# A hybrid trunk layer in which HGRN's key-value products share the scores' pair of PSUM banks and seven heads' outputs are scaled a step later

## The chip, the core and the metric

The kernel runs on one core of one Trainium2 chip. The metric is device time in microseconds (us); less is better. A core has TensorE (PE, with its weight loads as PEld), VectorE (DVE), ScalarE (ACT), GpSimd (POOL) and SyncE (SP), which here only issues DMAs. Each engine works through its own instructions in a fixed order and waits on semaphores for the others. PE writes into PSUM, of which the kernel uses eight banks of 128 partitions × 512 float32; DVE and ACT read the banks out.

## The reference

One decoder layer on x of 1024 tokens × 1024 channels, float32. Its token mixing has two branches, HGRN2 (8 heads, key and value width 128) and a retention (4 heads), which are gated, merged and projected; a squared-ReLU MLP follows. The change concerns HGRN2, whose recurrence in the reference goes over chunks of 64 tokens:

```python
def step(state, blk):
    qc, lfc, kc, vc = blk
    b = jnp.cumsum(lfc, axis=2)
    rel = jnp.where(causal, b[:, :, :, None, :] - b[:, :, None, :, :], -jnp.inf)
    scores = jnp.einsum('bhid,bhijd,bhjd->bhij', qc, jnp.exp(rel), kc)
    b_last = b[:, :, -1:, :]
    o = (jnp.einsum('bhij,bhje->bhie', scores, vc)
         + jnp.einsum('bhid,bhde->bhie', qc * jnp.exp(b), state))
    state = (jnp.exp(b_last[:, :, 0, :, None]) * state
             + jnp.einsum('bhjd,bhje->bhde', kc * jnp.exp(b_last - b), vc))
    return state, o
...
o = _head_norm(_from_chunks(o), centered=False).reshape(B, S, HG_WIDTH)
return (o * jax.nn.silu(g.astype(f32))).astype(g.dtype)
```

`_head_norm` divides each token's 128 outputs of a head by the root of their mean square. Scores, outputs and states of a head are what the words "scores", "outputs", "products" and "state" mean below; a product is the key-value sum that is added to the decayed state.

## The kernel before, in words

The dense projections run as three passes over hi and lo halves of the float32 operands (`mm3`, L188 to L190), in groups of 24 matmuls of 128x512 into a bank "d". Weights arrive in float32 and are split by ACT (L183) and DVE (L184). PSUM is handed out by `ps` under four letters, each with a number of banks that its tiles take in turn: "d" 3, "a" 2, "b" 1, "c" 2. A tile takes the bank of the tile that many places before it under the same letter, and its first write waits until that one's readers are done. In SBUF a pool of 15 half-row tiles (`e`) rotates in the same manner; loads that take such a tile wait until its last reader is done.

HGRN works in chunks of 128 tokens, eight of them a head, one head after another. `h_levels` computes a head's scores with the decay inside the chunk taken up level by level. The first level (L883) and two more (L935) are 32 small matmuls each, in which four groups of 32 rows work on one "a" bank; DVE copies the wanted entries out under a mask (L886, L887, L941) into a tile C. The last level (L923) fills two "a" banks of 32 small matmuls in all, which ACT copies out (L927). Between the levels DVE rescales queries and keys (L908 to L955).

`h_states` then takes the head's eight chunks in turn. For chunk n PE adds query times state (L991) and scores times values (L992) into a "c" bank `po`; ACT copies that out (L993) and squares it with a sum over each token (L994). For all but the last chunk PE multiplies turned keys and values (L997) into a bank `pu`, also "c", and DVE makes the new state of it: a copy for the first chunk (L1000), else old state times decay plus product (L1002). The keys are turned by four transposes (L973) into the "b" bank, once for each half of four chunks, and copied out by ACT (L975); the half's gate is loaded from DRAM by SP (L969).

At a half's last chunk DVE scales the mean squares (L1007) and POOL raises them to the power −1/2 (L1008). Two steps then follow with delays, counted in steps of the stream: `h_scale`, in which ACT scales the four output tiles (L1014), and `h_out`, in which PE transposes them into the "b" bank (L1024), DVE multiplies by the gate (L1028) and POOL stores them (L1029). The table `H_DEFER` holds both delays, one pair for heads 0 to 6 and one for head 7 (`H_DEFER[h // 7]`).

`h_stream` runs nine steps a head: at each step one chunk of the head before, one part of the levels of this head, then `tick`, which releases what is due. The stream is mixed at build time with dense projections (`h_fill`), the projection of the retention's finished outputs (`r_first`, L1341 and L1342) and the beginning of the retention's second head (`r_head`, whose loads of rq and rk are L1155 and whose transposes of the keys are L1167, into "a"). That is the order in which the program is written; a scheduler then sets each engine's final order from the instructions' dependences, its own estimates of their durations, and the order written. Instructions outside this stage keep their order in the change.

Of the kernel before, what the change touches and what calls it, by code (L numbers as in the profile page):

```python
# [19 lines left out]
P = 128  # L20
# [37 lines left out]

ADA_ORDER = [(s, g) for s in (S_GATE2, S_GATE1, S_SCALE2, S_SHIFT2) for g in range(4)]

H_DEFER = ((1, 2), (2, 3))
H_STEPS = 9


# [70 lines left out]
class Trunk:  # L135
# [824 lines left out]
    def h_states(self, p, hd):  # L960

        nc = self.nc
        h = 2 * p + hd
        s = self.hst[p][hd]
        k, v, Q, S, Dt = s["k"], s["v"], s["Q"], s["S"], s["D"]

        def turned(hf):
            g = self.e2()
            nc.sync.dma_start(g, self.hg_d[h][:, hf * 512:hf * 512 + 512])  # L969
            pb = self.ps("b")  # L970
            for c in range(4):
                cs = slice(hf * 512 + c * P, hf * 512 + c * P + P)
                nc.tensor.transpose(pb[:, c * P:(c + 1) * P], k[:, cs], self.ident)  # L973
            kt = self.e2()
            nc.scalar.activation(kt, pb, AF.Copy)  # L975
            return g, kt

        state = None
        nxt = turned(0)
        yield  # L980
        for hf in (0, 1):
            g, kt = nxt
            ob, sq = (self.e2().rearrange("p (c e) -> p c e", c=4) for _ in (0, 1))
            mr = self.xp.tile([P, 8], F32, tag="ms", bufs=2, name=self.uid("ms"))
            ms, rs = mr[:, :4], mr[:, 4:]
            for c in range(4):
                n = 4 * hf + c
                vn = v[:, n, hd * P:(hd + 1) * P]
                po = self.ps("c", (P, P))
                if n > 0:  # L990
                    nc.tensor.matmul(po, Q[hf][:, c * P:(c + 1) * P], state, start=True, stop=False)  # L991
                nc.tensor.matmul(po, S[:, n, :], vn, start=n == 0, stop=True)  # L992
                nc.scalar.activation(ob[:, c, :], po, AF.Copy)  # L993
                nc.scalar.activation(sq[:, c, :], ob[:, c, :], AF.Square, accum_out=ms[:, c:c + 1])  # L994
                if n < 7:
                    pu = self.ps("c", (P, P))
                    nc.tensor.matmul(pu, kt[:, c * P:(c + 1) * P], vn, start=True, stop=True)  # L997
                    ns = self.xp.tile([P, P], F32, tag="st", bufs=2, name=self.uid("st"))
                    if n == 0:
                        nc.vector.tensor_copy(ns, pu)  # L1000
                    else:
                        nc.vector.scalar_tensor_tensor(ns, state, Dt[:, n:n + 1], pu, op0=ALU.mult, op1=ALU.add)  # L1002
                    state = ns
                if n == 2:
                    nxt = turned(1)
                if c == 3:
                    nc.vector.tensor_scalar(ms, ms, 1.0 / P, HEAD_EPS, op0=ALU.mult, op1=ALU.add)  # L1007
                    nc.gpsimd.tensor_tensor(rs, ms, self.mhalf[:, :4], op=ALU.pow)  # L1008
                    self.later(H_DEFER[h // 7][0], lambda ob=ob, rs=rs, hf=hf, g=g: self.h_scale(h, hf, ob, rs, g))
                yield  # L1010

    def h_scale(self, h, hf, ob, rs, g):
# [4 lines left out]
        self.h_last = r  # L1017
        self.later(H_DEFER[h // 7][1], lambda: self.h_out(h, hf, ob, g))

# [856 lines left out]
```

## Time and profile before

| | us |
|---|---|
| median of 3 runs (2230.02 to 2231.53) | 2231.18 |
| the profiled execution | 2231.17 |
| its span in the profile | 2229.4 |
| PE busy outside the HGRN stage's later part, 0 to 912 us | 893.37 |
| PE busy from 1181 us to the end | 1032.34 |

The span leaves out 1.8 us around the profiled work. The last two rows are sums over windows of the profile: PE was busy for 893 of the first 912 us, and for 1032 of the last 1048. The mean granted clock of PE was 0.997 of full speed. A profile gives for each engine the time that it was busy, groups of instructions by source line and tile names (buffer numbers left out), the idle time before an instruction with the instruction that released it, and windows with the busy time and clock inside each. A group's "x64" counts records: a float32 matmul has two passes, and so two records.

### The profile page before, as it was taken

The page shows a single profiled execution, that of the slowest core. Times are in us where ns is not written, and L with a number is a line of the kernel's source. Part 1 is how long each engine was busy: PE and PEld are TensorE (multiplying, and loading weights), DVE is VectorE, ACT ScalarE, POOL GpSimd, SP SyncE. Part 2 cuts the span into 40 slices and gives each one's busy share as a digit, 9 for nine tenths or more (in the row PEclk, how much of TensorE's full clock was granted, in tenths as well). Part 3 has the DMA queues.
Part 4 walks back from the last instruction along what each step waited for, and adds up shares of the span by engine and source line. Part 5 has one row for each costly group of instructions (what it writes and reads, how often), then busy time and mean ns, then how long its engine had stood idle before and what let it go on. Part 6 is the DMA issues. An engine that isn't in the chain of part 4 may idle for free.

```text
span 2229.4 us, 32724 instructions
## 1 busy us (share of the span) xinstructions
PE 2188.0 (98%) x11879; PEld 1798.3 (81%) x11879; DVE 1577.7 (71%) x2756; ACT 1050.6 (47%) x1954; POOL 302.4 (14%) x468
## 2 busy tenths in 40 slices
PE   7999999999999999999999999999999999999998
PEld 5888888888888887888787888888888888788886
DVE  7866768686777637767756656687796665667778
ACT  5433334544333435555656545223565555643441
POOL 0111111011111113010022222031111211100001
PEclk9999999999999999999999999999999999999999
DMA  9766755543333355222237657764344444877863
GB/s 285 236 227 229 243 191 172 170 147 114 107 110 102 136 176 199 91 86 91 90 121 247 225 180 272 241 212 135 111 156 156 151 149 154 303 249 255 257 216 118
DMA packets 229378, 396.29 MB, mean 178 GB/s; under 512 B 17992, under 2 KB 123200, under 8 KB 228448
## 3 DMA queue, kind: packets, MB, share of 16 engines
q1 hardware_dynamic: 198464, 294.34, 41.3%
q0 software_dynamic: 30576, 99.79, 12.1%
q8 instruction: 93, 1.52, 0.3%
q14 instruction: 69, 0.57, 0.1%
q10 hardware_dynamic: 176, 0.06, 0.0%
HBM read 289.26 MB, written 104.87 MB: 177 GB/s over the span
## 4 chain that ended last, share of the span: by engine, by line
PE 88%; issue 3%; DVE 3%; DMA 2%; ACT 2%; POOL 1%; SPq 0%; DVEq 0%; ACTq 0%; POOLq 0%
PE psd L188 17%; PE psd L189 17%; PE psd L190 17%; PE psa L188 5%; PE psa L189 5%; PE psa L190 5%; PE psc L189 3%; PE psc L188 3%; PE psc L190 3%; PE psb L1247 2%; PE psb L188 2%; PE psb L189 2%; PE psb L190 1%; PE psc L1233 1%; PE psa L1181 1%
## 5 line engine op out<-in xcount | busy, mean ns | idle before, releaser
L188 PE MATMUL psd<-U,wh 128*128 128x512 f32 x696 | 279.3, 404 | 0.8 <-ACT U L183 0.7
L189 PE MATMUL psd<-U,wh 128*128 128x512 f32 x696 | 275.7, 396 | 0.3 <-DVE U L184 0.3
L190 PE MATMUL psd<-U,wl 128*128 128x512 f32 x696 | 275.2, 396 | 0.0
L183 ACT ACTIVATE bh<-s 128x512 fp32r<-128x512 f32 x212 | 133.1, 633 | 252.7 <-PE psd L189 64.6
L188 PE MATMUL psd<-U,bh 128*128 128x512 f32 x528 | 205.5, 389 | 2.0 <-DVE e L450 2.0
L183 ACT ACTIVATE bh<-raw 128x512 fp32r<-128x512 f32 x159 | 100.9, 637 | 224.2 <-PE psd L189 92.7
L189 PE MATMUL psd<-U,bh 128*128 128x512 f32 x528 | 205.5, 389 | 0.1
L190 PE MATMUL psd<-U,bl 128*128 128x512 f32 x528 | 205.4, 389 | 0.0
L184 DVE TENSOR_TENSOR bl<-raw,bh 128x512 fp32r<-128x512 f32 x159 | 108.5, 689 | 121.5 <-ACT bh L183 121.0
L184 DVE TENSOR_TENSOR bl<-s,bh 128x512 fp32r<-128x512 f32 x212 | 144.4, 686 | 64.9 <-ACT bh L183 64.9
L188 PEld LDWEIGHTS psd<-U,wh 128*128 128x128 f32 x696 | 131.3, 189 | 28.0 <-ACT U L183 2.8
L190 PEld LDWEIGHTS psd<-U,wl 128*128 128x128 f32 x696 | 131.8, 189 | 27.1
L189 PEld LDWEIGHTS psd<-U,wh 128*128 128x128 f32 x696 | 132.0, 190 | 26.9 <-DVE U L184 1.7
L183 ACT ACTIVATE U<-hr 128x512 fp32r<-128x512 f32 x112 | 70.3, 630 | 146.2 <-issue 75.5
L188 PEld LDWEIGHTS psd<-U,bh 128*128 128x128 f32 x528 | 99.1, 188 | 23.4 <-DVE e L450 2.8
L189 PEld LDWEIGHTS psd<-U,bh 128*128 128x128 f32 x528 | 99.1, 188 | 21.0 <-DVE U L184 0.5
L190 PEld LDWEIGHTS psd<-U,bl 128*128 128x128 f32 x528 | 99.1, 188 | 20.5
L184 DVE TENSOR_TENSOR U<-hr,U 128x512 fp32r<-128x512 f32 x112 | 77.0, 688 | 53.8 <-ACT U L183 53.4
L183 ACT ACTIVATE wh<-raw 128x512 fp32r<-128x512 f32 (+1 forms) x79 | 57.1, 740 | 101.3 <-PE psd L189 84.0
L188 PE MATMUL psa<-U,bh 128*128 128x512 f32 x264 | 102.9, 390 | 0.8 <-ACT e L438 0.8
L189 PE MATMUL psa<-U,bh 128*128 128x512 f32 x264 | 102.7, 389 | 0.0
L190 PE MATMUL psa<-U,bl 128*128 128x512 f32 x264 | 102.7, 389 | 0.0
(453 smaller groups left out, 5437.6 us busy)
## 6 DMA issues: line engine op xcount, KB each, us to landing
raw<-in_w_in SPq DMA_DIRECT2D x146, 512.0 KB, 4.3
raw<-in_w_down SPq DMA_DIRECT2D x64, 512.0 KB, 4.0
raw<-in_w_ada SPq DMA_DIRECT2D x32, 512.0 KB, 4.7
raw<-in_w_up SPq DMA_DIRECT2D x32, 512.0 KB, 3.9
raw<-in_w_pb SPq DMA_DIRECT2D x20, 512.0 KB, 4.4
v_d<-e POOLq DMA_DIRECT2D x32, 256.0 KB, 4.4
rg_d<-e POOLq DMA_DIRECT2D x32, 256.0 KB, 2.6
e<-v_d SPq DMA_DIRECT2D x32, 256.0 KB, 5.0
```

What stands on the lines that cost most here:

```text
L183: self.nc.scalar.activation(hi, src, AF.Copy)
L184: self.nc.vector.tensor_tensor(lo, src, hi.bitcast(F32), op=ALU.subtract)
L188: r = mm(out, wh, uh, start=start, stop=False, skip_group_check=more)
L189: mm(out, wh, ul, start=False, stop=False, skip_group_check=more)
L190: return r, mm(out, wl, uh, start=False, stop=stop, skip_group_check=more)
L1181: m = nc.tensor.matmul(pa[:, cs], k[e][:, cs], q[e][:, cs], start=e == 0, stop=e == 1)
L1233: mm(G[e], l[:, n % 2, es], r, start=n == 0 and i == 0, stop=i == 2, skip_group_check=n > 0)
L1247: mm(po, l, r, start=i == 0, stop=i == len(pairs) - 1)
```

## The change

Two edits. The product's bank `pu` is taken from the letter "a" instead of "c": the "a" pair then holds scores and products in turn, and the "c" pair the chunk outputs alone (and, after this stage, what the retention puts there). And the delay of `h_scale` of heads 0 to 6 goes from one step to two; that of `h_out` behind it stays at two, and head 7 is as before.

```diff
-H_DEFER = ((1, 2), (2, 3))
+H_DEFER = ((2, 2), (2, 3))
...
                 if n < 7:
-                    pu = self.ps("c", (P, P))
+                    pu = self.ps("a", (P, P))
                     nc.tensor.matmul(pu, kt[:, c * P:(c + 1) * P], vn, start=True, stop=True)
```

No instruction is added or removed. The scheduler gives PE, DVE, ACT, POOL and SP new orders within the HGRN stage. Three places on PE; a name's number counts tiles, and "x21" is a run of equal rows.

PE where chunks 2 and 3 of head 0's states run beside a level of head 1's scores (L935). Before:

```order
L997 MATMUL psc_8335<-U_7793,e_8145 128x128
L935 MATMUL psa_8367<-U_7790,fk_7802 32x48 x21
L991 MATMUL psc_8358<-st_8337,e_8130 128x128
L992 MATMUL psc_8358<-U_7793,U_7785 128x128
L935 MATMUL psa_8367<-U_7790,fk_7802 32x48 x10
L997 MATMUL psc_8363<-U_7793,e_8264 128x128
L935 MATMUL psa_8367<-U_7790,fk_7802 32x48
```

And in the changed kernel:

```order
L997 MATMUL psa_8335<-U_7793,e_8145 128x128
L997 MATMUL psa_8359<-U_7793,e_8264 128x128
L188 MATMUL psd_8417<-U_296,wh_7975 128x512
L189 MATMUL psd_8417<-U_297,wh_7975 128x512
L190 MATMUL psd_8417<-U_296,wl_7976 128x512
L991 MATMUL psc_8354<-st_8337,e_8130 128x128
L992 MATMUL psc_8354<-U_7793,U_7785 128x128
L935 MATMUL psa_8363<-U_7790,fk_7802 32x48 x32
```

The second product moves up to the first, three dense matmuls come between it and the next output, and the level's 32 matmuls stand in one piece.

PE where head 6's states begin, head 7's first scores (L883) are computed, and the outputs of head 5's second half are transposed (L1024); psd is a dense projection. Before:

```order
L992 MATMUL psc_10757<-U_7794,U_7785 128x128
L997 MATMUL psc_10761<-U_7794,e_10709 128x128
L883 MATMUL psa_10765<-hq_7792,fk_10496 32x3x16 x32
L1024 MATMUL psb_10800<-cst,e_10525 128x128 x4
L188 MATMUL psd_10808<-U_10714,wh_10268 128x512
```

And in the changed kernel:

```order
L992 MATMUL psc_10757<-U_7794,U_7785 128x128
L997 MATMUL psa_10761<-U_7794,e_10705 128x128
L883 MATMUL psa_10765<-hq_7792,fk_10492 32x3x16 x32
...
L190 MATMUL psd_10800<-U_10729,wl_10265 128x512
L991 MATMUL psc_10816<-st_10763,e_10690 128x128
L992 MATMUL psc_10816<-U_7794,U_7785 128x128
L997 MATMUL psa_10821<-U_7794,e_10705 128x128
L1024 MATMUL psb_10834<-cst,e_10521 128x128 x4
```

The transposes move behind twelve dense matmuls (the last of them is shown) and the next chunk's output and product.

PE near the end of the stage, where the retention's keys are transposed (L1167) into two "a" banks behind the last head's products. Before:

```order
L997 MATMUL psc_11295<-U_7794,e_11163 128x128
L1167 MATMUL psa_11301<-cst,e_11211 128x128
L1167 MATMUL psa_11301<-cst,e_11212 128x128
L1167 MATMUL psa_11301<-cst,e_11211 128x128
L1167 MATMUL psa_11301<-cst,e_11212 128x128
L1167 MATMUL psa_11308<-cst,e_11211 128x128
```

And in the changed kernel, in which psa_11308 has the bank that psa_11295 had:

```order
L997 MATMUL psa_11295<-U_7794,e_11159 128x128
L1167 MATMUL psa_11301<-cst,e_11203 128x128
L1167 MATMUL psa_11301<-cst,e_11204 128x128
L1167 MATMUL psa_11301<-cst,e_11203 128x128
L1167 MATMUL psa_11301<-cst,e_11204 128x128
L188 MATMUL psd_11334<-U_10714,wh_10734 128x512
L1167 MATMUL psa_11308<-cst,e_11203 128x128
```

A dense matmul now stands between the two groups of four.

## The prediction

> **What bounds the kernel now.** I read the page first: how busy each engine is, and the chain of work that ended last.
>
> ```profile
> span 2229.4 us, 32724 instructions
> PE 2188.0 (98%) x11879; PEld 1798.3 (81%) x11879; DVE 1577.7 (71%) x2756; ACT 1050.6 (47%) x1954; POOL 302.4 (14%) x468
> PE 88%; issue 3%; DVE 3%; DMA 2%; ACT 2%; POOL 1%; SPq 0%; DVEq 0%; ACTq 0%; POOLq 0%
> ```
>
> TensorE (PE) is busy for 98% of the span and carries 88% of the chain. So an edit is worth what it takes from PE: idle time of PE, time that PE runs at a lower clock, or PE time spent badly. Next, the stage that the change touches, from about 912 to 1181 us, as a whole and around its longest wait. Columns: window; its length; then busy us and count of PE, weight loads, DVE, ACT, POOL; the granted PE clock; DMA share; GB/s.
>
> ```profile
> 912.00:1181.00 269.00, 262.27 (x2988) 217.80 (x2988) 172.77 (x395) 151.30 (x451) 37.66 (x46) 0.99 0.30 100
> 1117.00:1119.00 2.00, 1.77 (x7) 1.15 (x8) 0.53 (x1) 1.62 (x7) 0.59 (x1) 0.97 0.29 113
> 1119.00:1122.20 3.20, 3.20 (x9) 2.49 (x8) 3.06 (x9) 0.00 (x0) 0.55 (x1) 0.50 0.24 93
> 1122.20:1126.00 3.80, 3.80 (x21) 3.25 (x20) 0.47 (x3) 1.17 (x4) 0.54 (x1) 0.99 0.18 69
> ```
>
> PE is idle for 269.00 − 262.27 = 6.7 us of the stage; DVE is busy 64% and ACT 56% of it, so neither is a bound over the stage. From 1119.0 to 1122.2 PE ran at clock 0.50. Then PE's waits in the same window (us in total, times, longest):
>
> ```profile
> PE psb L1024 <- ACT e L1014: 3.2, 3, 1.7
> PE psc L991 <- DVE st L1002: 1.2, 4, 0.5
> PE psc L997 <- ACT e L975: 1.1, 3, 0.6
> PE psa L923 <- DVE U L955: 0.5, 1, 0.5
> PE psa L935 <- DVE U L909: 0.3, 1, 0.3
> ```
>
> These are 6.3 of the 6.7 us. The longest, followed back through the timelines (start, duration, then the idle time before it and who ended it):
>
> ```profile
> 1114.34 0.39 PE L997 MATMUL psc<-U,e 128*128 128x128 f32 x2
> 1114.66 0.89 PE L883 MATMUL psa<-hq,fk 128*32 128x48 f32 x64
> 1117.23 1.21 PE L1024 MATMUL psb<-cst,e 128*128 128x128 f32 x4 [1.69 <-ACT e L1014]
> 1114.57 0.16 DVE L1007 TENSOR_SCALAR ms<-ms 128x4 f32<-128x4 f32 x1
> 1114.82 1.92 POOL L1008 TENSOR_TENSOR ms<-ms,small 128x4 f32<-128x4 f32 x1 [9.79 <-DVE ms L1007]
> 1116.78 1.28 ACT L1014 ACTIVATE e<-e,ms 128x128 f32<-128x128 f32 x4 [1.85 <-POOL ms L1008]
> ```
>
> The chain is DVE L1007, then 1.92 us of POOL's power L1008, then ACT's scaling L1014, then the transposes. PE reached the transposes at 1117.23 − 1.69 = 1115.54 and stood for 1.69 us, and the half clock follows right behind.
>
> **Change, part 1: scaling a step later.** The order of this place is the second of those shown with the change: the transposes leave the place right behind L883. Twelve dense matmuls and a chunk's three products (L991, L992, L997) now run first. What that is worth, from the rows:
>
> ```profile
> 959.08 0.39 PE L189 MATMUL psd<-U,wh 128*128 128x512 f32 x1
> 959.30 0.39 PE L190 MATMUL psd<-U,wl 128*128 128x512 f32 x1
> 959.53 0.38 PE L991 MATMUL psc<-st,e 128*128 128x128 f32 x2
> 959.75 0.39 PE L992 MATMUL psc<-U,U 128*128 128x128 f32 x2
> 959.97 0.39 PE L997 MATMUL psc<-U,e 128*128 128x128 f32 x2
> ```
>
> A dense matmul starts 0.22 to 0.23 us after the one before, and so does a product (two passes each). Twelve and three are 15 × 0.225 = 3.4 us of new cover against a wait of 1.69. The other two waits sum to 3.2 − 1.7 = 1.5 us, each under it. **Term: −3.2 us** (bounds 0 and −3.2).
>
> With the wait goes the half clock. The window at 1119.0 has 3.20 us at 0.50, that is 1.6 us of work lost. **Term: −1.6** (bounds 0 and, with the transposes that ran into it, −2.1). The page "TensorE: Matmul & The Clock Gate" of the Trainium skill, in Part 1, has the gate look at activity in free-running windows of 3413 ns, and its closing table ("Why this matters for your kernels") asks only that no idle gap exceed about 3 us; by that rule a gap of 1.69 us costs no clock, the term is nothing, and the sum would be 1.6 us smaller. The trace disagrees as to the size: here 0.50 stands behind 1.69 us.
>
> The scaling's other effects: as many ACT instructions are issued as before, and the transposes, DVE's multiplication by the gate (L1028) and POOL's store (L1029) come a step later, off the chain. But the scaled tile, the gate tile and their rotating places in the pool of 15 come free later. The order on SP shows one consequence: the retention's load of rq (L1155) now takes the place of head 6's second output tile, and so waits for its transposes; behind it on SP queue one rq, two rk and hg loads.
>
> ```profile
> 1151.67 1.01 SPq L1155 DMA_DIRECT2D e<-rk_d  x2
> 1159.11 1.04 PE L1167 MATMUL psa<-cst,e 128*128 128x128 f32 x8
> ```
>
> Before, 6.4 us lay between the last rk issue (1152.68) and the transposes L1167 of the retention's keys that read it, and L1167 waited for nothing. How early the loads landed inside those 6.4 us is not seen here, and the group of transposes that they now wait for takes 0.6 to 1.2 us (1.21 at the half clock above): I take **+0.8**, nearer to the side of no wait (bounds 0 and +3, if the whole 6.4 us were needed and the issue came half a step of PE's work later).
>
> **Part 2: the products move to the scores' banks.** Before, outputs and products shared two "c" banks, so every product waited for the copy of the output before it and each output for a state update; now the outputs have both. The products (L997) take turns with the scores (L883, L935, L923) in two "a" banks. The first order shown with the change has what follows.
>
> A product no longer waits behind an output's copy, so it is issued early, and the small score matmuls stay in one piece. The price of splitting them is in the trace; a whole set first, then one that two groups of products split:
>
> ```profile
> 891.79 0.89 PE L935 MATMUL psa<-U,fk 128*32 128x48 f32 x64
> 892.61 0.50 PE L188 MATMUL psd<-U,wh 128*128 128x512 f32 x1
> ...
> 960.29 0.70 PE L935 MATMUL psa<-U,fk 128*32 128x48 f32 x42
> 961.17 0.49 PE L991 MATMUL psc<-st,e 128*128 128x128 f32 x2 [0.18 <-DVE st L1002]
> 961.50 0.39 PE L992 MATMUL psc<-U,U 128*128 128x128 f32 x2
> 961.81 0.45 PE L935 MATMUL psa<-U,fk 128*32 128x48 f32 x20
> 962.19 0.49 PE L997 MATMUL psc<-U,e 128*128 128x128 f32 x2
> 962.61 0.27 PE L935 MATMUL psa<-U,fk 128*32 128x48 f32 x2
> 962.81 0.50 PE L188 MATMUL psd<-U,wh 128*128 128x512 f32 x1
> ```
>
> In one piece the 64 passes take 892.61 − 891.79 = 0.82 us. Split twice they and three products take 962.81 − 960.29 = 2.52 us; less 0.82, less three products at 0.22, less the idle 0.18, 0.86 us are left, 0.43 for each interruption. Counted over the stage, the order has the scores in 59 pieces before and 44 after. Most of the fifteen cut a set as here, some move only an edge, so I take 0.32 each: **−4.9** (bounds: nothing, if the time belongs to the products, and 15 × 0.43 = −6.4).
>
> The three waits of L997 for L975 (the copy of the turned keys) sum to 1.1 us. After the change those products find the copy done, since PE does other things first: **−1.1** (bounds 0, −1.1). The four waits of L991 for the state update L1002 sum to 1.2 us. By start-to-start times of the rows above, 14 of 56 places before have under 0.8 us of PE work between product and the next use of the state, 4 after. In the group at 923 us three instructions, not one, delay the state:
>
> ```profile
> 923.30 0.63 ACT L183 ACTIVATE wh<-raw 128x512 fp32r<-128x512 f32 x1 [5.38 <-PE psd L189]
> 923.97 0.69 DVE L184 TENSOR_TENSOR wl<-raw,wh 128x512 fp32r<-128x512 f32 x1 [1.76 <-PE psc L992]
> 924.58 0.34 DVE L1002 SCALAR_TENSOR_TENSOR st<-st,D,psc 128x128 f32<-128x128 f32 x1
> ```
>
> The update stood behind the weight's split (L184), so some of the wait stays: **−0.6** (bounds 0, −1.2).
>
> **New waits on the "a" pair.** A product now waits for DVE's masked copies of the scores that held its bank, and scores wait for the update that reads a product. The longest such reads:
>
> ```profile
> L941 DVE COPY_PREDICATED hC<-mask,psa 128x128 f32<-128x128 uint8 x42 | 13.2, 315 | 3.1 <-PE psa L935 3.0
> ```
>
> Three copies are 0.95 us; the order leaves at least 2.2 us of PE work (estimated from the rows' start-to-start times) between scores and the product that takes their bank, at 14 places. An update is 0.34 us; the order leaves 0.45 and 0.9 us at the two tightest of 14 places where L923 follows, and one dense matmul, 0.23 us, besides the first group ahead of the second group of transposes L1167 (the third order shown). I put 0.4 on that last, 0.3 on the 0.45, 0.3 on the rest: **+1.0** (bounds 0 and +6, that is 0.4 at each of the 15). Behind a product that waits, PE holds everything.
>
> **Sum**: −3.2 −1.6 −4.9 −1.1 −0.6 +0.8 +1.0 = −9.6 us. The profiled execution took 2231.17 us and the median of the runs is 2231.18, so the sum applies unchanged: **2221.5 us**.
>
> **Rivals.** *The gain is mostly hidden.* The time in the split sets belongs to the products that follow small matmuls and not to the split, or the fewer pieces come back as waits on banks. Then −4.9 falls away and new waits cost 2 us more: −9.6 + 4.9 + 2.0 = −2.7, **2228.5 us**. For it: this one split set carries the price. Against: the split set's own pieces are longer, passes and products alike (0.49 against 0.39).
>
> *The "a" pair becomes the tight resource.* This one ends slower. It decides when DVE finishes the third masked copy later than 2.2 us behind the scores: three copies (0.95) and one weight split (0.69) in its queue make 1.64 and fit; a second split ahead of them, 2.33, is just too late, and a third operation of that length makes it 3.02 and the wait 0.8. Then 14 products behind L935 wait 0.8 us each, 11.2, the 7 behind L883 (with two copies to wait for) half of that, 2.8, and two such waits end in a half clock, 3.2 us. With −11.4 from what is removed and +0.8 from the loads, that is +6.6: **2238 us**. In "Perfetto Trace Analysis", section "Matmuls", the Trainium skill has independent matmul groups rotate through different banks, so that reading one out overlaps the next group; by that, putting three kinds of work in one pair speaks against this change, and the sum would be this rival's. The trace bears it out only in part: L935 and L923 waited 0.8 us in all before, and never for a bank.
>
> *The deferral does nothing*: DVE issues L1007 later behind its copies, POOL's power ends as much later, and PE stands again where the transposes are now. Then 3.2 + 1.6 stay: −4.8, **2226.4 us**. Against: L1007 would have to slip by the 3.4 us of new cover, ten times an update's 0.34.
>
> **How the numbers follow.** Forecast, including the cases near it, 0.64; deferral without effect 0.05; hidden 0.21; tight pair 0.10. The forecast's own ends: all gains at their bounds and no new wait, −3.2 − 2.1 − 6.4 − 1.1 − 1.2 = −14, 2217; the tops of the new waits in part, about 2227. The range reaches to 2215.5 below, for a wait that goes without being counted here (L923 and L935, 0.8), and to 2231 above, past the hidden rival. A measurement of this kernel can tell about 0.2%, 4.5 us, from no change, so faster means under 2226.7: 0.68. Same, between 2226.7 and 2235.6: 0.23. Slower: 0.09.
>
> **What would show it.** In the profile after: no wait of L1024 for L1014 in the stage before head 7; no half clock near 1120 us; L935 rows of x64 in most groups, and the stage's end (L1167 behind it) about 9 us earlier. A row "psa L997 <- DVE hC" of over 5 us would show the tight pair; a wait of L1167 for the rq or rk load the SP term. The forecast is wrong if PE's busy time in the stage doesn't fall by 4 us or more: then the pieces were no cost.

## The result and the profile after

The changed kernel takes 2218.26 us (median of 3 runs, 2217.57 to 2218.39), before 2231.18: a ratio of 0.9941, 95% interval 0.9928 to 0.9955, some 12.9 us less. Of all the runs in this document one, of the deferral alone, took 3789.64 us at a mean granted clock of 0.634, for a cause that isn't known; the ratios leave it out, and the median of that kernel's other ten is 2226.48. The profile of the changed kernel is of an execution of 2217.57 us. Its page, span, busy time by engine and the chain by engine:

```profile
span 2215.8 us, 32734 instructions
PE 2180.3 (98%) x11879; PEld 1792.3 (81%) x11879; DVE 1575.5 (71%) x2756; ACT 1049.3 (47%) x1954; POOL 301.5 (14%) x468
PE 90%; DVE 3%; DMA 3%; ACT 2%; issue 1%; POOL 0%; SPq 0%; DVEq 0%; ACTq 0%; POOLq 0%
```

The same work takes 7.7 us less of PE's busy time (2188.0 before), and the span is 13.6 us shorter. To see both on equal terms, one window each from the stage's first L883 to the same PE instruction near its end; first before, then after (columns as in the prediction):

```profile
886.67:1174.27 287.60, 280.87 (x3303) 232.33 (x3303) 190.51 (x433) 156.99 (x465) 36.28 (x44) 0.99 0.31 102
```

```profile
887.19:1161.85 274.66, 273.39 (x3304) 227.19 (x3304) 190.28 (x433) 156.29 (x465) 34.97 (x44) 1.00 0.33 108
```

The stretch is 12.94 us shorter. Its idle time of PE fell from 287.60 − 280.87 = 6.73 to 1.27, by 5.5 us. Its busy time fell by 7.5; 1.7 of that is the half clock, which the stretch of before has once (3.41 us at 0.50) and that of after not at all. 5.8 us are left: the same matmuls, done in less time. PE's waits in the stage after (912 to 1170 us):

```profile
PE psc L991 <- DVE st L1002: 0.5, 1, 0.5
PE psc L991 <- DVE st L1000: 0.5, 1, 0.5
```

Nothing else is left of the 6.3 us of before, and no wait names a bank. The place where PE stood for 1.69 us, in the timeline of after:

```profile
1107.20 0.89 PE L883 MATMUL psa<-hq,fk 128*32 128x48 f32 x64
1108.02 0.50 PE L188 MATMUL psd<-U,wh 128*128 128x512 f32 x1
...
1111.32 0.39 PE L997 MATMUL psa<-U,e 128*128 128x128 f32 x2
1111.54 0.60 PE L1024 MATMUL psb<-cst,e 128*128 128x128 f32 x4
1111.89 0.48 PE L188 MATMUL psd<-U,wh 128*128 128x512 f32 x1
```

The transposes start without an idle time behind the dense matmuls and products, and take 0.35 us. And a whole score set beside the chunk's products, where before had it in three pieces:

```profile
959.98 0.89 PE L935 MATMUL psa<-U,fk 128*32 128x48 f32 x64
960.80 0.49 PE L991 MATMUL psc<-st,e 128*128 128x128 f32 x2
961.12 0.39 PE L992 MATMUL psc<-U,U 128*128 128x128 f32 x2
961.35 0.39 PE L997 MATMUL psa<-U,e 128*128 128x128 f32 x2
```

The 64 passes take 0.82 us, with one way in and one way out. The retention's loads, which now wait for a tile of head 6, and the transposes that read them:

```profile
1133.02 1.71 SPq L1155 DMA_DIRECT2D e<-rq_d  x2
1136.33 4.41 SPq L1155 DMA_DIRECT2D e<-rk_d  x2
```

```profile
1146.92 0.60 PE L1167 MATMUL psa<-cst,e 128*128 128x128 f32 x4
1147.27 0.48 PE L188 MATMUL psd<-U,wh 128*128 128x512 f32 x1
1147.60 0.60 PE L1167 MATMUL psa<-cst,e 128*128 128x128 f32 x4
```

The last rk load is issued by 1140.74, 6.2 us ahead of L1167, and L1167 waits for neither the load nor the bank.

### The profile page after: what moved, and what is told of

It reads as the page before. It is cut to its first block, busy times and chain, and to the rows that moved or that the text cites. A ratio compares the mean times of both kernels' runs of the same rounds, so it can differ in the third digit from the quotient of the medians.

```text
span 2215.8 us, 32734 instructions
## 1 busy us (share of the span) xinstructions
PE 2180.3 (98%) x11879; PEld 1792.3 (81%) x11879; DVE 1575.5 (71%) x2756; ACT 1049.3 (47%) x1954; POOL 301.5 (14%) x468
## 4 chain that ended last, share of the span: by engine, by line
PE 90%; DVE 3%; DMA 3%; ACT 2%; issue 1%; POOL 0%; SPq 0%; DVEq 0%; ACTq 0%; POOLq 0%
PE psd L188 17%; PE psd L189 17%; PE psd L190 17%; PE psa L190 5%; PE psa L189 5%; PE psa L188 5%; PE psc L189 3%; PE psc L188 3%; PE psc L190 3%; PE psb L1247 2%; PE psb L188 1%; PE psb L189 1%; PE psb L190 1%; PE psc L1233 1%; PE psa L1181 1%
## 5 line engine op out<-in xcount | busy, mean ns | idle before, releaser
L183 ACT ACTIVATE bh<-s 128x512 fp32r<-128x512 f32 x212 | 133.2, 633 | 253.2 <-PE psd L189 65.5
L183 ACT ACTIVATE bh<-raw 128x512 fp32r<-128x512 f32 x159 | 100.9, 637 | 224.0 <-PE psd L189 92.4
L184 DVE TENSOR_TENSOR bl<-raw,bh 128x512 fp32r<-128x512 f32 x159 | 108.4, 689 | 121.1 <-ACT bh L183 120.5
L184 DVE TENSOR_TENSOR bl<-s,bh 128x512 fp32r<-128x512 f32 x212 | 144.4, 686 | 66.3 <-ACT bh L183 66.1
L183 ACT ACTIVATE U<-hr 128x512 fp32r<-128x512 f32 x112 | 70.4, 630 | 144.7 <-issue 75.5
L184 DVE TENSOR_TENSOR U<-hr,U 128x512 fp32r<-128x512 f32 x112 | 77.0, 687 | 53.0 <-ACT U L183 52.6
L183 ACT ACTIVATE wh<-raw 128x512 fp32r<-128x512 f32 (+1 forms) x79 | 57.1, 740 | 98.8 <-PE psd L189 79.8
```

Of the source, the lines that this page charges most:

```text
L183: self.nc.scalar.activation(hi, src, AF.Copy)
L184: self.nc.vector.tensor_tensor(lo, src, hi.bitcast(F32), op=ALU.subtract)
```

## The experiments

All ran beside runs of before. Their medians were 2231.17 us for the two single edits and the two kernels with split sets, 2232.30 for the two that move the step within the deferral, and 2231.26 for the other four. Edits are shown against the changed kernel unless said otherwise.

**Each edit alone.** The bank alone:

```diff
-H_DEFER = ((2, 2), (2, 3))
+H_DEFER = ((1, 2), (2, 3))
```

> The bank change alone; the scaling stays one step behind. Counted over the stage its order has the scores in 42 pieces (before 59, both edits 44). If the parts add as in my working, the fewer pieces and the waits of L991 and L997 are won here, about 5.7 and 2 us, and the waits of L1024 for L1014 stay, about 3 us, with a half clock behind one of them or not: 2223 to 2224. Rival, the deferral does nothing: as fast as both edits, 2218. Rival, the pieces are no cost: 2228 to 2229.

2227.15 us, ratio 0.9982 (0.9973 to 0.9991). That misses the expected range by 3.2 us and lies nearer to the rival by which the pieces are no cost; the windows below and the pair with the extra product speak against that rival. The deferral alone:

```diff
-                    pu = self.ps("a", (P, P))
+                    pu = self.ps("c", (P, P))
```

> The deferral alone; the products stay in the outputs' banks. 60 pieces of scores, as before. If the parts add: the waits of L1024 for L1014 go, 3.2 us, and up to 3.4 us of lost clock with them, while the waits of L991 and L997 stay: 2225 to 2228. Rival, the deferral does nothing: 2231.

2226.89 us, ratio 0.9978 (0.9969 to 0.9987), within the expected range. The windows of the same stretch, the bank alone first, then the deferral alone:

```profile
885.73:1166.55 280.82, 274.77 (x3303) 226.79 (x3303) 190.62 (x433) 156.55 (x465) 36.09 (x44) 1.00 0.31 106
```

```profile
886.33:1168.04 281.71, 278.69 (x3304) 231.09 (x3303) 190.89 (x433) 156.22 (x465) 35.84 (x44) 1.00 0.31 105
```

The two edits take from different columns. Without the half clock, before has 280.87 − 1.71 = 279.16 us of busy PE. The bank takes 4.4 us of it (42 pieces) and leaves 6.05 us idle; the deferral takes 0.5 (60 pieces) and leaves 3.02 us idle. Of PE's waits with the bank alone, up to 1160 us, those of the transposes are the longest:

```profile
PE psb L1024 <- ACT e L1014: 4.1, 3, 1.7
```

These were 3.2 us before: PE comes to the transposes sooner (for head 1's first half 0.8 us after DVE starts the last L1007, and 1.5 in before), while POOL's power ends 1.8 us after that start in both, so part of what the banks win is lost again in the wait that the other edit removes. The profiled execution of the bank alone was the fastest of its eleven runs (2223.24), so its window says which column moves, and the median how much.

**Is the whole more than the parts?** The kernel with both edits once more:

> The kernel with both edits, unchanged, beside the runs of before on one chip, to set against each edit alone (4.0 and 4.3 us by the medians). If both edits together are worth more than the sum, as the first comparison has it (12.9 against 8.3): 2217 to 2219. If that was the luck of three runs: 2222 to 2223.

2219.16 us, ratio 0.9949 (0.9937 to 0.9962), in the first of the expected ranges but for 0.2 us. The product of the ratios of the two single edits is 0.9960, and the intervals overlap; so by the medians a gain beyond the sum is likely, but its size isn't shown. In the windows of the stretch the parts take 4.4 + 0.5 us of busy time and 0.7 + 3.7 of idle time, both edits together 5.8 and 5.5: 2.0 us beyond the sum, of which the longer wait of the bank alone (4.1 against 3.2) is 0.9.

**What a split set costs.** Two kernels with the same extra work, an identity product into unused columns of each of 24 score banks, in front of the set or in its middle:

```diff
+    def extra(self, n, r, pw):
+        if r == 0 and n == 0:
+            x = self.nc.tensor.matmul(pw[:, 384:512], self.ident, self.ident, start=True, stop=True)
...
+            pw = self.ps("a")
+            pa = pw[:, :384]
...
+                    self.extra(n, r, pw)
```

For the middle, `n == 4`, and the product is put behind the score matmul before it; in both the next score matmul is put behind the product.

> Both edits, and in each of the 24 sets of 32 small score matmuls (L883, L935) one extra 128x128 product of the identity with itself into unused columns of the set's bank, ahead of the set's first matmul. It is the base for the next run. 24 extra products at 0.22 us are 5.3 us, and no further interruption of a set (42 pieces): 2223 to 2225, by every theory.

> As the run before it, but the extra product stands in the middle of each set, so that the sets are in 68 pieces and not 42; the work is the same. If an interruption of a set costs 0.32 to 0.43 us, as the split set of the trace has it, this is 26 times that, 8 to 11 us, over the run with the extra products in front. Rival, the time in the split sets belongs to the products and not to the split: the same as that run within 1.5 us.

In front 2225.71 us (ratio 0.9976, 0.9966 to 0.9987), 0.7 above its expected range; in the middle 2229.98 (0.9996, 0.9987 to 1.0005). The split costs 4.3 us end to end, which is neither of the expected outcomes: about half of the lower figure of the first, and clear of the rival's 1.5. The windows say why, in front first:

```profile
886.30:1166.62 280.32, 278.22 (x3349) 232.35 (x3349) 190.40 (x432) 156.26 (x465) 36.14 (x44) 1.00 0.31 105
```

```profile
886.67:1172.95 286.28, 286.22 (x3351) 236.09 (x3351) 191.09 (x433) 156.72 (x465) 35.18 (x44) 1.00 0.31 104
```

PE's busy time rose by 8.00 us for 26 more pieces, 0.31 us each, at the full clock in both. But the slower PE no longer waits at all in this stretch: 0.06 us idle against 2.10, so 2.0 us of the price came back there. The rest of the difference lies behind the stretch and was not followed further. So the rival, that the time belongs to the products, falls: the same products and the same small matmuls cost 8 us more when interleaved. What in the change from one to the other takes the 0.31 us isn't shown.

**What the deferral does, PE's order or ACT's?** The extra step put behind the scaling instead of ahead of it; PE's order stays row for row that of both edits, and on ACT the scaling may come earlier:

```diff
-H_DEFER = ((2, 2), (2, 3))
+H_DEFER = ((1, 3), (2, 3))
```

> Both edits in their effect on PE, whose order is the same row for row, but with the extra step put behind the scaling and not ahead of it (delays 1 and 3 for 2 and 2): ACT issues L1014 as early as before, and waits there for POOL. If the later place of the transposes on PE is all that matters: as both edits, 2218 to 2220. If it matters that ACT doesn't stand at L1014 while splits and copies wait behind it: 1 to 4 us slower, with waits of PE for ACT's L975 or L183, or for DVE behind them.

2218.63 us, ratio 0.9939 (0.9925 to 0.9953), as both edits. And the reverse, in which the transposes stay as near to the outputs as before:

```diff
-H_DEFER = ((2, 2), (2, 3))
+H_DEFER = ((2, 1), (2, 3))
```

> The scaling a step later, the transposes a step sooner after it (delays 2 and 1), so that the transposes stand where they stood before; products in the scores' banks. If the cover ahead of the transposes is what the deferral brings, the waits of L1024 for L1014 return, four or more, 5 us and over: 2225 to 2229, as the bank change alone or slower. Rival, a later scaling alone is enough: 2219.

2226.07 us, ratio 0.9973 (0.9961 to 0.9985). The waits for L1014 from 885 to 1185 us, first of the scaling early and the transposes late, then of the transposes near (1.6 us in each is head 7's last, which before had too):

```profile
PE psb L1024 <- ACT e L1014: 1.6, 1, 1.6
```

```profile
PE psb L1024 <- ACT e L1014: 5.6, 4, 1.7
```

What counts is how much other work PE has ahead of the transposes. On ACT the scaling's place hardly differs between these kernels: by the traces, with both edits the first three of a half's four scalings stand where they stand with delays 1 and 3, and only the fourth comes 1 to 5 us later, in eight of the fourteen halves of heads 0 to 6. So a scaling that is late on ACT was not tried, and nothing is shown of it.

**A step more.**

```diff
-H_DEFER = ((2, 2), (2, 3))
+H_DEFER = ((3, 2), (2, 3))
```

> Both edits, and the scaling of heads 0 to 6 one step later again (delays 3 and 2). No wait of L1024 for L1014 was left in the heads concerned, so nothing is to be won there: within 1.5 us of both edits, 42 pieces instead of 44 may be worth 0.6.

A miss: 2223.61 us, ratio 0.9969 (0.9958 to 0.9979), 4.5 us over both edits on the same chip. The timelines around the new wait:

```profile
1088.18 0.99 ACT L1014 ACTIVATE e<-e,ms 128x128 f32<-128x128 f32 x3 [3.60 <-POOL ms L1008]
1089.07 1.99 ACT L183 ACTIVATE U<-onr 128x1024 fp32r<-128x1024 f32 x2
1090.14 1.23 DVE L184 TENSOR_TENSOR U<-onr,U 128x1024 fp32r<-128x1024 f32 x1 [2.89 <-ACT U L183]
1092.76 0.69 DVE L909 TENSOR_TENSOR U<-U,D 128x512 f32<-128x512 f32 x1
1093.59 0.89 PE L935 MATMUL psa<-U,fk 128*32 128x48 f32 x64 [2.69 <-DVE U L909]
```

Here ACT stands 3.60 us at the scaling, waiting for POOL; the split of the retention's outputs (L183) is queued behind it, DVE's half of the split (L184) behind that, the rescaling L909 in DVE's queue behind that, and PE's scores last. PE loses 2.69 us, with a half clock behind it. The number of pieces (42) didn't help.

That ACT stands there is not new: with both edits the same scaling stands 1.80 us, with the same split behind it. Two things differ; the rows with a step more first, then with both edits:

```profile
1084.68 0.60 POOL L1029 DMA_DIRECT2D oh_d<-e  x1 [13.57 <-DVE hC L941]
1085.34 2.80 POOL L1008 TENSOR_TENSOR ms<-ms,small 128x4 f32<-128x4 f32 x1
1091.62 1.22 DVE L184 TENSOR_TENSOR U<-onr,U 128x1024 fp32r<-128x1024 f32 x1
```

```profile
1085.67 1.39 POOL L1008 TENSOR_TENSOR ms<-ms,small 128x4 f32<-128x4 f32 x1 [6.86 <-DVE ms L1007]
1087.09 0.99 ACT L1014 ACTIVATE e<-e,ms 128x128 f32<-128x128 f32 x3 [1.80 <-POOL ms L1008]
1090.21 0.68 DVE L909 TENSOR_TENSOR U<-U,D 128x512 f32<-128x512 f32 x1
1090.81 1.22 DVE L184 TENSOR_TENSOR U<-onr,U 128x1024 fp32r<-128x1024 f32 x1
```

The power took 2.80 us instead of 1.39, right behind a store that stands 7.4 us ahead of it with both edits; whether the store made it longer isn't shown. From L1007's start to ACT's scaling that is 1.5 us more. And DVE runs the second of its two instructions for the split (L184, 1.22 us) ahead of L909, where both edits have it behind: from the scaling to L909 another 1.5 us. These 3 us make the wait, in this one profile; the longer power and DVE's new order did it, and not a later scaling as such.

**Outputs in the scores' banks instead of products.**

```diff
-                po = self.ps("c", (P, P))
+                po = self.ps("a", (P, P))
...
-                    pu = self.ps("a", (P, P))
+                    pu = self.ps("c", (P, P))
```

> The other way round: the chunk outputs share the scores' pair and the products have the c pair alone; the deferral stays. 46 pieces of scores (44 with both edits). If only the parting of outputs and products matters: 2218 to 2220. If what shares the scores' pair matters, since an output's bank must wait for three of ACT's copies (L927, 1.1 us) with 0.9 us of PE work between in three heads: waits of L991 for L927, 0.5 to 1 us at three to seven places, 2221 to 2226.

2221.81 us, ratio 0.9966 (0.9953 to 0.9978): at the lower end of the second range, but not for its reason. No wait of L991 for L927 shows; L991 waits three times, 0.8 us in all, and only the L993 of these rows reads a bank that the next output takes:

```profile
PE psa L991 <- DVE D L911: 0.4, 1, 0.4
...
PE psa L991 <- ACT e L993: 0.2, 1, 0.2
PE psa L991 <- DVE st L1000: 0.2, 1, 0.2
```

The stretch is 277.16 us long here against 274.95 in the second profile of both edits; 1.75 of these 2.2 us are busy time, with 46 pieces against 44, of which two pieces at 0.31 explain 0.6. Parting outputs from products is most of what the bank edit adds to the deferral, whichever of them goes to the scores; no long wait for the pair of banks shows in either.

**The wait that is left,** 1.6 us of head 7's last transposes:

```diff
-H_DEFER = ((2, 2), (2, 3))
+H_DEFER = ((2, 2), (3, 3))
```

> Both edits, and the scaling of head 7 one step later as well (delays 3 and 3 for 2 and 3). Its last transposes then stand behind twelve more dense matmuls, 2.7 us of cover for the wait of 1.6 us that is left for L1014; half clocks behind that wait go too. 1.6 to 3.3 us under both edits: 2215 to 2217. Rival, the later store of the outputs holds up their loads for the projection: as both edits, or slower.

2220.48 us, ratio 0.9952 (0.9940 to 0.9965): a miss, no better than both edits. The wait is gone and another stands at its place. PE's timeline, both edits first, then this run:

```profile
1175.79 0.66 PE L1024 MATMUL psb<-cst,e 128*128 128x128 f32 x4 [1.58 <-ACT e L1014]
```

```profile
1177.47 0.97 PE L188 MATMUL psd<-U,wh 128*128 128x512 f32 x3 [2.24 <-ACT U L183]
```

The dense matmuls that were to be its cover need ACT's split of the loaded outputs (L183, at 1176.37), which isn't ready either: the transposes had stood ahead of a wait of nearly the same length. That is the number of the rival but not its reason, since the split waits for no load. ACT comes to it late, behind an instruction (L1249) that itself had stood 1.58 us waiting for PE. No version beat the changed kernel by more than the measurement tells.

## Why the prediction was right

The time, 2218.26 us, lies in the range; the forecast was 3.2 us too high, and its likeliest case is the one that came.

- *The waits of L1024 for L1014*, −3.2: none is left ahead of head 7. The two runs with the step moved within the deferral show that the later place on PE does it, by the cover that I counted.
- *The half clock*, −1.6: 1.71 in the stretch. That it stood there at all was partly the luck of the profiled execution: the bank alone keeps a wait of 1.68 us at the same transposes and has no half clock behind it (the last section says why). A second one of before, behind head 7's wait, is missing from the profile after as well, though that wait is still there; that is the same luck, my sum did not have it, and its 1.7 us cover the 1.2 us that the profiles differ behind the stretch.
- *Fewer pieces*, −4.9: the term was mis-sized by a little. Busy time without the half clock fell by 5.8 us. The price of one, taken as 0.32, measured 0.31 in the pair with the extra product; so not all of the 5.8 can be pieces (15 × 0.31 = 4.6), and where the other 1.2 came from was not isolated. By the bank alone it is less: 17 fewer took 4.4, or 0.26 each. The deferral alone took 0.5 of busy time without fewer pieces, and with the products moved, the kernels that keep the waits of L1024 have 274.6 to 274.8 us of it in 42 pieces (the bank alone; the transposes near, less its half clock), those that lost them 273.4 to 274.0 in 44. So about 1 us goes with the later transposes; by what is open.
- *L997 waiting for L975*, −1.1: gone. *L991 waiting for L1002*, −0.6: one wait of 0.5 is left of 1.2, and one for L1000 of 0.5 is new.
- *The retention's loads*, +0.8, and *new waits on the "a" pair*, +1.0: neither came; the wait for L1000 (0.5) is one on the state. These two terms, with the waits of L923 and L935 (0.8) that I left standing and that went, are 2.1 us of the 3.2.
- *The rivals.* "Hidden" falls by the pair with the extra product, "the deferral does nothing" by the deferral alone. The tight pair falls: no wait for an "a" bank shows in the profile of both edits, and one of 0.2 us where the outputs take the products' place. The rule in the Trainium skill's "Perfetto Trace Analysis", section "Matmuls", on rotating independent groups through different banks, fits what did pay, parting products from outputs; that three kinds of work in one pair would collide, as I read out of it, did not happen.

## What to carry to other kernels

On an engine that is nearly always busy, look not only for its waits but for how often small work of one kind is cut by work of another: here each cut of a set of small matmuls cost 0.31 us, and a bank letter decided how many cuts the scheduler made. A delay for a slow chain is worth its wait only while useful and ready work stands ahead of the consumer; one step more changed the scheduler's orders on POOL and DVE, made a new wait elsewhere, and lost 4.5 us. And speeding up the engine that arrives at a wait lengthened that wait here, from 3.2 to 4.1 us, so two edits of which one removes the wait belong in one trial.

## What was not expected of the hardware

The half clock keeps to a fixed grid. By the trace's clock records, it began in the execution of before at 1118.90 and 1190.58 us, 3.413 us long each time, and in that of the third deferral at 1094.41 and 1179.74: 71.68 and 85.33 us apart, which are 21.0 and 25.0 times 3.413. In the other profiles with two, the end of the execution counted, the distance is a whole number of 3.413 us too. The same wait of 1.6 us at head 7's last transposes stands in eleven profiles and is followed by a half clock in seven of them. A half clock is 1.7 us of lost work; that it moves the time between runs of one kernel is likely and not shown: the one kernel with two traces, that with both edits, has no half clock in either.

The traces say more on what decides. I laid the grid of each execution over PE's rows and summed the idle time in each of its windows of 3.413 us, from 25 to 2205 us. The window just ahead of each of the twelve half clocks (those at the end left out) holds 1.5 to 2.6 us of it. No window with less is followed by one, but eight windows with 1.57 to 1.88 us are not followed either, so this is no sharp limit. In three of the four profiles without a half clock behind head 7's wait the grid cuts the wait, and no window there holds over 1.3 us; in the fourth, the deferral alone, one holds 1.58, and why it was spared is open. In the same way the grid cuts the wait of 1.68 us of the bank alone into 1.06 and 0.62, while before's 1.69 us lie in one window.

The Trainium skill's page "TensorE: Matmul & The Clock Gate", Part 1, has free-running windows of 3413 ns, and the traces agree. Its closing table, "Why this matters for your kernels", asks for no idle gaps over about 3 us; here that was not enough, since waits of 1.6 and 1.69 us had a half clock behind them.
